# Second layer's memory heads of a two-layer encoder: TensorE's order written out, values in passes of two tiles, and copies first in the stage of sums

## The chip, the cores and the metric

The kernel runs on one core of one Trainium2 chip, as one launch. The metric is the device time of a run in microseconds (us); a lower time is better. The kernel before takes 1526.08 us, the median of three runs (1525.7 to 1526.91).

## The reference

A trunk of two layers over 1024 tokens of width 1024, with 256 memory tokens beside them, all in float32. The first layer has global, windowed and memory heads, the second has neighbourhood and memory heads. What matters here is the second layer:

```python
h = rmsnorm(x, norm_gain[l])
qc, kc, vc, qm, gate = split_cols(h @ w_in_odd[o], SPLIT_ODD)   # 16 heads of 64, 4 of 128, a gate of 1536
yc = neighborhood_attn(qc, kc, vc, rpb_c[o])
ym = memory_attn(qm, mk, mv)           # 4 heads of 128 against 256 memory tokens
y = concat([yc, ym]) * silu(gate)
x = x + y @ w_out_odd[o]

def memory_attn(q, mk, mv):
    s = einsum('bshd,bmhd->bhsm', q, mk) * 128 ** -0.5
    p = softmax(s, axis=-1)
    return einsum('bhsm,bmhd->bshd', p, mv)
```

## The kernel before, in words

**Matmuls.** Every matrix product is made of three `fp32r` matmuls on a high and a low half of each operand: high by high, high by low, low by high. The high half is a rounding copy (`copy`, L112, ScalarE), the low half is the value minus it (VectorE or GpSimd). "Projection of a tile" means 128 output features for all tokens: 2 x 8 steps of three matmuls of 512 columns (`token_steps`, L213 to 230, matmul at L224), into a PSUM bank called `pj`. Activations lie in SBUF as `H`, 16 tiles.

**What sets the order.** A scheduler places each engine's instructions by program order and by priorities: `AHEAD` (L31 to 38) gives each phase a table of names with offsets, and `with self.ahead("evict")` (L81) raises what it encloses by that much. `issue_after` ties an instruction behind another one. An engine wrapped in `Pinned` (L51 to 58) keeps its instructions in program order. Work that is to fill gaps is written as generators in `self.waiting`, and `pull(n)` (L203) issues n steps of them behind the last scores or transposes (`self.fence`).

**Stages.** `prep`; the first layer (`l0`); its output projection (`out0`); `front`; `l1`, which calls `odd`; the last output projection (`out1`). The change touches two:

*`front` (L1374 to 1581), the stage of sums.* It projects the second layer's gates and memory queries by pairs of tiles with sums and differences of the operands, so that seven block products stand for eight. Early products (`x`, `z`) and the values of tiles 0 and 1 (`values_of_two`, L402) run while the operands are still being made (`operands`, L1393); at its start the row sums `rows` of the norm are added (L1656, in `done`), while `weights()` (L1504) splits the next weight tiles. Then a loop (L1540 to 1581) goes over seven pairs in the order 0, 1, 2, 5, 6, 3, 4 (5 and 6 are the memory queries). Each pair has four products into the banks `y`, `x`, `y`, `x` and a last one into `z`; `product` is at L1441. Between them ScalarE copies a bank to SBUF (`c22`, `c12`, `c21`, tiles called `P`), under the priority "sink" (20), VectorE adds (`plus`), and `end` (L1444) finishes a block: gates go through tanh, queries are split into halves, and a DMA stores them. `z` is a new allocation of the single bank `pv`; `x` has five banks.

*`odd` (L1770 to 1821), first part: the opening.* Four memory heads run with the projection of values beside them. `values_of_two` projects value tiles 2 and 3 for all tokens (192 matmuls of 256 columns, weights split into two tiles called `v`, bank `pj`); `values` (L373) projects tiles 4 to 7 at once (192 matmuls of 512 columns, weights in `k` and `v` tiles). Both wait as fill, with the query projection `q0` behind them. `mem_att` (L560) does a head in two groups of four 128-token blocks. For each half group, two blocks: scores into a bank `s` (two buffers; L579 to 581), maximum (L583) and its scaling by `-scale` (L591) on VectorE, exponentials on ScalarE (L594), reciprocal (L598), normalisation on GpSimd (L600), then `pull(1)`. For the whole group then, twice: four transposes into a bank `tr` (`flip`, L120), copy to `ph` and difference `pl` (`p_parts`, L481 to 488), `pull(1)`, three products into `pv` (L611 to 613). At the end of a group `pv` is copied to `y`, and at the end of a head `gated_rows` (L476) multiplies by the gate and stores. Nothing holds TensorE's instructions in this order; the scheduler picks them.

*`odd`, second part.* Eight pairs of neighbourhood heads (`near_head`, L1012), each with the projections of the next pair's keys and queries as fill.

**Tiles.** `k` has eight buffers, `q` four, `v` two, `ph` and `pl` four each; the banks `s`, `tr`, `pv`, `pj` two each. The tag `P` is an alias of `k` in this phase.

Of the kernel before, what the change touches and what calls it, by code (L numbers as in the profile page):

```python
# [23 lines left out]
UNIT = 4  # L24

# [35 lines left out]
class Trunk:  # L61
# [8 lines left out]
    def __init__(self, tc, io):  # L70
        self.tc = tc
        self.nc = tc.nc
        self.io = io
        self.n = 0
        self.bufs = {}
        self.pools = {}
        self.alias = {}
        self.raw = False
        self.later, self.waiting, self.copies = None, deque(), deque([], 8)

# [37 lines left out]
    def flip(self, outs_ins):  # L118
        for o, i in outs_ins:
            self.turned = self.fence = self.nc.tensor.transpose(o, i, self.ident)  # L120
# [91 lines left out]

    def token_steps(self, w, nt, moving, cols, sink):  # L213

        nc = self.nc
        ws = [self.wunit(w[nt, :, u * UNIT * 128:(u + 1) * UNIT * 128]) for u in range(KT // UNIT)]
        for c, n in cols:
            a = self.ps("pj")
            for kt in range(KT):
                h, l = ws[kt // UNIT]  # L220
                mh, ml = moving(kt, c, n)
                with self.ahead("proj"):
                    for i, (s, m) in enumerate(((h, mh), (h, ml), (l, mh))):
                        nc.tensor.matmul(a[:, :n], s[:, kt % UNIT, :], m, start=(kt == 0 and i == 0),  # L224
                                         stop=(kt == KT - 1 and i == 2))
                if kt < KT - 1:
                    yield
            with self.ahead("sink"):
                sink(a, c, n)
            yield  # L230
# [142 lines left out]
    def values(self, w, vd, g):  # L373

        nc = self.nc
        hs = [self.st("k", [128, 2, 512], F32R) for _ in range(4)]
        ls = [self.st("v", [128, 4, 512], F32R) for _ in range(2)]
        ws = [(hs[kt // 2][:, kt % 2, :], ls[kt // 4][:, kt % 4, :]) for kt in range(KT)]
        for kt, (h, l) in enumerate(ws):
            with self.ahead("w"):  # L380
                raw = self.wload(w[4 * g:4 * g + 4, :, kt * 128:(kt + 1) * 128].rearrange("h p n -> p h n"))
                self.copy(h, raw)
                (nc.gpsimd if kt % 2 else nc.vector).tensor_tensor(l, raw, h, op=OP.subtract)
        yield
        for b in range(8):
            p = self.ps("pj")
            t = slice(b * 128, b * 128 + 128)
            for kt, (h, l) in enumerate(ws):
                for i, (x, m) in enumerate(((self.h[0], h), (self.h[0], l), (self.h[1], h))):
                    nc.tensor.matmul(p, x[kt][:, t], m, start=(kt + i == 0), stop=(kt == KT - 1 and i == 2))  # L390
                if kt % 4 == 3:
                    yield
            for e in range(2):
                o = self.st("ph", [128, 2, 2, 2, 64], F32R)
                src = p[:, e * 256:(e + 1) * 256].rearrange("p (j h d) -> p j h d", j=2, h=2)
                with self.ahead("evict"):
                    self.copy(o[:, :, :, 0, :], src)
                    nc.vector.tensor_tensor(o[:, :, :, 1, :], src, o[:, :, :, 0, :], op=OP.subtract)
                    nc.sync.dma_start(vd[2 * g + e][:, :, b, :].rearrange("j p n -> p j n"),
                                      o.bitcast(F32).rearrange("p j h e d -> p j (h e d)"))  # L400

    def values_of_two(self, w, vd, tag, bank, out, pieces=1):  # L402
# [5 lines left out]
        for k in range(0, KT, 2):  # L408
            h, l = hs[k // 2], ls[k // 2]
            with self.ahead("w"):  # L410
# [4 lines left out]
                (nc.vector if pieces > 1 else nc.gpsimd).tensor_tensor(l4, raw, h4, op=OP.subtract)  # L415
        yield
        for b in range(0, 8, 2):
            p = self.ps(bank[b // 2 % len(bank)])
            for e in range(2):
                t = slice((b + e) * 128, (b + e) * 128 + 128)  # L420
                for kt in range(KT):
                    for i, (x, m) in enumerate(((0, hs), (0, ls), (1, hs))):
                        self.last = nc.tensor.matmul(p[:, 256 * e:256 * e + 256], self.h[x][kt][:, t], m[kt // 2][:, kt % 2, :],
                                                     start=e + kt + i == 0, stop=kt == KT - 1 and i == 2,
                                                     skip_group_check=True)
                    if kt % 4 == 3 and (e == 0 or kt < KT - 1):
                        yield
# [8 lines left out]
            yield  # L436
# [123 lines left out]
    def mem_att(self, q, kv):  # L560
        nc = self.nc
        scale = 128.0 ** -0.5
        qh, ql = q
        kh, kl = kv[:, 0, :], kv[:, 1, :]
        vh, vl = (kv[:, i, :].rearrange("p (c d) -> p c d", c=2) for i in (2, 3))
        y = self.st("yb", [128, T])
        wide = "p_sa" in self.bufs
        nb = 4 if wide else 2
        behind = list(self.copies) if wide else []
        for g in range(2):  # L570
            pt = self.st("P", [128, 4, MEM])
            st = self.tiny()
            for i in range(0, 4, nb):
                s = self.ps("sa", (128, T)) if wide else self.ps("s")
                with self.ahead("score"):
                    for b in range(nb):
                        q = slice((g * 4 + i + b) * 128, (g * 4 + i + b + 1) * 128)
                        o = s[:, b * MEM:(b + 1) * MEM]
                        nc.tensor.matmul(o, qh[:, q], kh, start=True, stop=False)  # L579
                        nc.tensor.matmul(o, qh[:, q], kl, start=False, stop=False)  # L580
                        self.fence = nc.tensor.matmul(o, ql[:, q], kh, start=False, stop=True)
                with self.ahead("exp"):
                    nc.vector.tensor_reduce(st[:, i:i + nb], s.rearrange("p (b k) -> p b k", b=nb), axis=AX.X,  # L583
                                            op=OP.max)
                    blk = g * 4 + i
                    raw = self.raw
                    if raw:
# [1335 lines left out]
```

## Time and profile before

| | |
|---|---|
| median of three runs | 1526.08 us (1525.7 to 1526.91) |
| the profiled execution's own time | 1532.29 us |
| its span | 1530.5 us |
| instructions in the span | 24962 |
| TensorE busy | 1484.7 us, 8221 matmuls and transposes |
| VectorE busy | 1051.3 us |
| ScalarE busy | 828.6 us |
| GpSimd busy | 665.1 us |
| mean granted TensorE clock | 0.99 |

How to read it: the profile shows one execution, with its span counted from the first to the last instruction; the execution's own time is 1.8 us more. "PE" is TensorE's matmuls, "PEld" its weight loads, "DVE" VectorE, "ACT" ScalarE, "POOL" GpSimd, "SP" the engine that issues most DMAs. A row of a waits view names the instruction that came after idle time of its engine (engine, output, line), what ended that time (engine, output, line), the idle time in us, how often, and the longest. A row of a windows view gives a stretch in us from the span's start, its length, and for PE, PEld, DVE, ACT and POOL the busy time and the number of instructions; then the granted TensorE clock as a share of full speed, the DMA engines' busy share, and GB/s. A row of a timeline gives start and duration in us, engine, line, operation, output and inputs, and in brackets a wait and what ended it. In these views `front` runs from about 785 to 968, the opening to about 1081, the neighbourhood heads follow.

### The profile page before, as it was taken

What the parts mean: (1) busy time and instruction counts of PE and PEld (TensorE: products, weight loads), DVE (VectorE), ACT (ScalarE), POOL (GpSimd) and SP (SyncE); (2) the same over time, 40 slices, a digit from 0 to 9 for tenths busy, and PEclk for the clock granted to TensorE, in tenths of its full rate; (3) what the DMA queues carried; (4) which work ended last, traced back from release to release, by engine and by line L of the source; (5) the groups of instructions that cost most, each with busy time, mean ns of one, the idle gap of its engine ahead of it and who ended that gap; (6) DMA issues with size and microseconds to landing.
All of it is one profiled execution on the core that took longest, in us unless ns stands there. A gap on an engine that the chain in (4) does not pass through costs nothing.

```text
span 1530.5 us, 24962 instructions
## 1 busy us (share of the span) xinstructions
PE 1484.7 (97%) x8221; PEld 1273.2 (83%) x8221; DVE 1051.3 (69%) x2263; ACT 828.6 (54%) x1822; POOL 665.1 (43%) x790
## 2 busy tenths in 40 slices
PE   9999999999999999999999999988999999999997
PEld 8798898988888788778878777977788888888886
DVE  6687777677676688776578865444477777777754
ACT  7743665655665456554454543443366666666552
POOL 1323547456654555433440001242255566664355
PEclk9999999999999999999999999999999999999998
DMA  8866324232323323287552434674555566678834
GB/s 291 287 163 183 98 70 138 83 118 86 108 90 103 111 84 121 80 283 250 193 171 83 163 116 137 218 236 149 175 166 183 185 206 204 205 214 292 297 121 136
DMA packets 166817, 252.47 MB, mean 165 GB/s; under 512 B 14752, under 2 KB 97952, under 8 KB 165664
## 3 DMA queue, kind: packets, MB, share of 16 engines
q1 hardware_dynamic: 166256, 250.80, 50.9%
q8 instruction: 65, 1.06, 0.3%
q14 instruction: 64, 0.52, 0.1%
q10 hardware_dynamic: 432, 0.09, 0.0%
HBM read 164.32 MB, written 74.45 MB: 156 GB/s over the span
## 4 chain that ended last, share of the span: by engine, by line
PE 82%; DMA 6%; DVE 5%; ACT 2%; issue 2%; POOL 2%; SPq 0%; POOLq 0%; ACTq 0%; DVEq 0%
PE pj L224 27%; PE tr L120 8%; PE pv L995 4%; PE pj L1198 3%; PE x L1441 3%; PE pv L1034 3%; PE sa L1198 3%; PE pj L784 3%; PE tr L1198 2%; PE s L1198 2%; PE pj L390 2%; PE y L1441 2%; PE pv L1441 2%; PE sa L962 2%; PE sa L963 2%
## 5 line engine op out<-in xcount | busy, mean ns | idle before, releaser
L224 PE MATMUL pj<-H,wh 128*128 128x512 f32 x1280 | 423.1, 411 | 1.2 <-DVE vt L313 0.9
L224 PE MATMUL pj<-H,wl 128*128 128x512 f32 x640 | 251.9, 394 | 0.0
L112 ACT ACTIVATE ph<-tr 128x512 fp32r<-128x512 f32 (+2 forms) x336 | 179.7, 539 | 130.8 <-PE tr L120 125.3
L224 PEld LDWEIGHTS pj<-H,wh 128*128 128x128 f32 x1280 | 220.4, 189 | 34.2 <-DVE vt L313 1.2
L487 DVE TENSOR_TENSOR pl<-tr,ph 128x512 fp32r<-128x512 f32 (+2 forms) x336 | 204.8, 615 | 49.7 <-ACT ph L112 47.6
L142 POOL TENSOR_SCALAR wh<-wraw 128x512 fp32r<-128x512 f32 x78 | 51.5, 663 | 284.5 <-DMA g<-P 160.9
L224 PEld LDWEIGHTS pj<-H,wl 128*128 128x128 f32 x640 | 120.2, 188 | 27.7
L112 ACT ACTIVATE wh<-wraw 128x384 fp32r<-128x384 f32 (+1 forms) x162 | 88.6, 552 | 94.3 <-PE tr L1198 16.0
L144 POOL TENSOR_TENSOR wl<-wraw,wh 128x512 fp32r<-128x512 f32 x82 | 106.8, 1304 | 29.9 <-ACT wh L112 25.7
L120 PE MATMUL tr<-ident,P 128*128 128x128 f32 x752 | 115.2, 273 | 1.5 <-DVE pl L487 0.9
L1152 POOL TENSOR_TENSOR wl<-wraw,wh 128x384 fp32r<-128x384 f32 x56 | 61.0, 1089 | 116.7 <-ACT wh L112 108.6
L970 POOL TENSOR_SCALAR P<-P,st 128x1024 f32<-128x1024 f32 x64 | 75.8, 1187 | 66.5 <-DVE st L969 66.4
L1065 POOL TENSOR_SCALAR pn<-pn,st 128x384 f32<-128x384 f32 (+1 forms) x128 | 73.4, 576 | 68.2 <-DVE st L1064 38.2
L1063 ACT ACTIVATE pn<-pn,st 128x384 f32<-128x384 f32 (+1 forms) x128 | 75.1, 587 | 42.6 <-DVE st L1062 36.8
L120 PEld LDWEIGHTS tr<-ident,P 128*128 128x128 f32 x752 | 88.6, 140 | 10.2 <-DVE pl L487 2.1
L968 ACT ACTIVATE P<-sa,st 128x1024 f32<-128x1024 f32 x64 | 71.5, 1117 | 43.3 <-DVE st L967 23.7
L967 DVE TENSOR_REDUCE st<-sa 128x1 f32<-128x1024 f32 x64 | 77.5, 1218 | 12.1 <-PE sa L963 9.4
L784 PE MATMUL pj<-ah,H 128*128 128x256 f32 x384 | 72.7, 286 | 1.0 <-DVE H L729 0.9
L1152 DVE TENSOR_TENSOR wl<-wraw,wh 128x384 fp32r<-128x384 f32 (+1 forms) x64 | 46.7, 730 | 30.4 <-ACT wh L112 30.1
L1059 DVE CUSTOM_DVE_ANT_0 pn<-s,bm 128x384 f32<-128x384 f32 x96 | 53.1, 554 | 20.2 <-PE tr L120 14.5
L995 PE MATMUL pv<-ph,va 128*128 128x256 f32 x256 | 66.6, 285 | 0.0
L995 PE MATMUL pv<-pl,va 128*128 128x256 f32 x256 | 65.8, 284 | 0.0
(502 smaller groups left out, 3912.8 us busy)
## 6 DMA issues: line engine op xcount, KB each, us to landing
wraw<-w_o SPq DMA_DIRECT2D x62, 256.0 KB, 3.7
y<-yb SPq DMA_DIRECT2D x24, 512.0 KB, 3.4
wraw<-s SPq DMA_DIRECT2D x64, 192.0 KB, 3.2
y<-sg SPq DMA_DIRECT2D x23, 512.0 KB, 3.6
wraw<-w_e SPq DMA_DIRECT2D x44, 256.0 KB, 3.0
k<-k SPq DMA_DIRECT2D x42, 256.0 KB, 4.3
wraw<-w_mem SPq DMA_DIRECT2D x32, 256.0 KB, 4.4
v<-v SPq DMA_DIRECT2D x8, 1024.0 KB, 5.1
```

The lines of the kernel that those rows point to most:

```text
L112: return self.nc.scalar.activation(out, in_, AF.Copy, scale=scale)
L120: self.turned = self.fence = self.nc.tensor.transpose(o, i, self.ident)
L144: e.tensor_tensor(lf, raw, hf, op=OP.subtract)
L224: nc.tensor.matmul(a[:, :n], s[:, kt % UNIT, :], m, start=(kt == 0 and i == 0), stop=(kt == KT - 1 and i == 2))
L487: nc.vector.tensor_tensor(pl[:, :n], tr[:, :n], ph[:, :n], op=OP.subtract)
L784: self.last = nc.tensor.matmul(a[:, b * 256:(b + 1) * 256], x[kt][:, t], w, start=(kt + b + i == 0), stop=(kt == KT - 1 and i == 2), skip_ ...
L967: nc.vector.tensor_reduce(st[:, 0:1], s, axis=AX.X, op=OP.max, negate=True)
L970: self.normal = nc.gpsimd.tensor_scalar(pt, pt, st[:, 2:3], 0.5, op0=OP.mult, op1=OP.mult)
L995: nc.tensor.matmul(o[:, :256], v[:, c + k, kv, :], part[:, k * 256:(k + 1) * 256], start=(c + k == 0 and part is parts[0]), stop=(c + k == ...
L1152: engine.tensor_tensor(lf, raw, hf, op=OP.subtract)
L1198: last = nc.tensor.matmul(bank, s[:, k, :], y[3 * u + k][m][:, cols], start=start and u + k + e == 0, stop=u == 1 and k + e == 4, skip_gro ...
L1441: self.last = nc.tensor.matmul(bank, ws[s][:, k, :], b[k][m], start=start and k + i == 0, stop=k == UNIT - 1 and i == 2, skip_group_check= ...
```

## The change

**Opening.** A new function `opening` takes the place of the first part of `odd`. TensorE is wrapped in `Pinned`, so that its instructions stand in the written order: scores of group 0; then for each group n the scores of group n + 1, the transposes and the products of group n. Behind each half group of scores and behind each set of transposes stands fill for `SLOT` = 5800 columns of matmul (a generator step now yields the columns that it issued, and `self.due` carries the rest over). Fill is, in order: the query projection `q0`; three value passes of two tiles (`values_of_two` for tiles 2 and 3 with weights in `v`; 4 and 5 in `k`, in two pieces; 6 and 7 in `v` again); the key projection `k0`; the query projection `q1`. A pass's weights are loaded and split one pass ahead. `values` is gone. The low halves of value weights are made on VectorE (before: on GpSimd for tiles 2 and 3, on both in turn for 4 to 7).

**Queries.** The factor 128^-0.5 is now applied to the memory queries where `front` stores them (`end`), so the exponential takes no scale, the maximum is negated as it is made, and the scaling on VectorE (L591) goes. Queries are loaded by groups of 512 columns, two groups ahead.

**Near heads.** What `opening` has made for the first pair is handed over; `q1` is used for the second pair, and the five steps of fill that the first pair had beside its own (`pull(5)`) go.

**Front.** `weights()` is tied behind the addition of the row sums (`self.squares`). The copies `c22`, `c12` and `c21` get the priority "evict" (500) for "sink" (20). For the pairs 5 and 6 the bank of the last product is a buffer of `x` for `pv`. The low halves of the early value weights stay on VectorE, now by an argument.

`mem_att` itself loses its narrow form (the first layer still calls it) and is cut into `mem_norm`, `mem_flips` and `mem_pv`. The diff, cut to its core:

```diff
+SLOT = 5800
...
     def token_steps(self, w, nt, moving, cols, sink):
-        ws = [self.wunit(w[nt, :, u * UNIT * 128:(u + 1) * UNIT * 128]) for u in range(KT // UNIT)]
+        ws = self.ready.pop(nt, None) or self.units(w, nt)
...
-                        nc.tensor.matmul(a[:, :n], s[:, kt % UNIT, :], m, start=(kt == 0 and i == 0),
+                        self.pe.matmul(a[:, :n], s[:, kt % UNIT, :], m, start=(kt == 0 and i == 0),
...
-                    yield
+                    yield 3 * n
...
-    def values(self, w, vd, g):
...
-    def values_of_two(self, w, vd, tag, bank, out, pieces=1):
+    def values_of_two(self, w, vd, tag, bank, out, pieces=1, low=None):
...
-                (nc.vector if pieces > 1 else nc.gpsimd).tensor_tensor(l4, raw, h4, op=OP.subtract)
+                (low or nc.gpsimd).tensor_tensor(l4, raw, h4, op=OP.subtract)
...
@@ front @@
             if kind == "mem":
-                self.split(o[:, 0, :], o[:, 1, :], p)
+                h, l = (o[:, i, :] for i in range(2))
+                self.copy(h, p, 128.0 ** -0.5)
+                nc.vector.scalar_tensor_tensor(l, p, 128.0 ** -0.5, h, op0=OP.mult, op1=OP.subtract)
...
-                    weights()
+                    with tc.issue_after(self.squares.ins):
+                        weights()
...
-            y, z = self.ps("y"), self.ps("pv")
+            y, z = self.ps("y"), self.ps("pv" if j < early else "x")
...
-            with self.ahead("sink"):
+            with self.ahead("evict"):
                 self.copy(c22, y)
...
-            with self.ahead("sink"):
+            with self.ahead("evict"):
                 self.copy(c12, x)
...
+            with self.ahead("evict"):
+                self.copy(c21, x)
             with self.ahead("sink"):
-                self.copy(c21, x)
                 plus(c22, x)
...
@@ done @@
-                        nc.vector.tensor_tensor(rows1, sums[0], sums[1], op=OP.add)
+                        self.squares = nc.vector.tensor_tensor(rows1, sums[0], sums[1], op=OP.add)
...
+    def opening(self, w, kvd, vd, mqd, gate, yd):
+        nc, tc = self.nc, self.tc
+        self.pe = Pinned(tc, nc.tensor)
+        with self.ahead("first"):
+            kvm = {0: self.load("k", kvd[0], (128, 4, MEM))}
+            load = lambda n: self.load("q", mqd[n // 2][:, :, n % 2 * 512:n % 2 * 512 + 512].rearrange("i p n -> p i n"), (128, 2, 512))
+            qs = deque(load(n) for n in range(2))
...
+        of_two = lambda k, tag, pieces: self.values_of_two(w[O_V + k:O_V + k + 2], vd[k // 2], tag, ("pj",), "ph", pieces, nc.vector)
+        def work():
+            a, b, c = of_two(2, "v", 1), of_two(4, "k", 2), of_two(6, "v", 1)
+            q0 = lazily("q0", lambda: self.q_pair(w, O_Q))
+            first = next(q0)
+            next(a)
+            yield first
+            yield from q0
+            next(b)
+            yield from a
+            next(c)
+            yield from b
+            made["bm"] = [self.near_bias(i) for i in range(2)]
+            k0 = lazily("k0", lambda: self.k_pair(w, O_K))
+            self.ready[O_K] = self.units(w, O_K)
+            yield from c
+            made["v"] = self.load("v", vd[0][0], (128, 8, 256)).rearrange("p b (h d) -> p b h d", h=2)
+            self.ready[O_Q + 1] = self.units(w, O_Q + 1)
+            yield from k0
+            yield from lazily("q1", lambda: self.q_pair(w, O_Q + 1))
+        todo = work()
+        def fill(cols):
+            self.due += cols
+            while self.due > 0:
...
+                self.due -= n
+        fill(16 * 1536)
+        def scores(n):
...
+            for i in range(0, 4, 2):
+                s = self.ps("s")
...
+                with self.ahead("exp"):
+                    nc.vector.tensor_reduce(st[:, i:i + 2], s.rearrange("p (b k) -> p b k", b=2), axis=AX.X, op=OP.max,
+                                            negate=True)
+                    for b in range(2):
+                        nc.scalar.activation(pt[:, i + b, :], s[:, b * MEM:(b + 1) * MEM], AF.Exp,
+                                             bias=st[:, i + b:i + b + 1], accum_out=st[:, 8 + i + b:9 + i + b])
+                    self.mem_norm(pt, st, i, 2)
+                fill(SLOT)
...
+        pt = scores(0)
+        for n in range(8):
...
+            now, pt = pt, scores(n + 1) if n < 7 else None
+            o = self.ps("pv")
+            for c in range(2):
+                parts = self.mem_flips(now, c)
+                fill(SLOT)
+                self.mem_pv(o, kvm[h], c, parts)
+            with self.ahead("close"):
+                self.copy(y[:, g * 512:(g + 1) * 512], o)
+            if g:
+                self.gated_rows(gate(8 + h), 8 + h, y, yd)
+        while not ("q1" in made):
+            fill(1)
...
+        self.pe = nc.tensor
+        return made
...
@@ odd @@
-        self.waiting += [self.values_of_two(w[O_V + 2:O_V + 4], vd[1], "v", ("pj",), "ph"), self.values(w[O_V:], vd, 1)]
...
+        made = self.opening(w, kvd, vd, mqd, gate, yd)
+        now = [made[k] for k in ("bm", "k0", "v", "q0")]
         side = self.weight_sums(self.io["w_oo"], sd, "mk", nc.gpsimd)
-        for h in range(4):
-            y = self.mem_att(mqs.pop(0), kvm)
...
         for j in range(8):
...
-                    now = qkv(j + 1)
+                    now = qkv(j + 1, None if j else made["q1"])
...
-            if j == 0:
-                self.pull(5)
```

167 lines of the change are left out of this document (78 added, 89 removed).

## The prediction, on record before the changed kernel had run

> **What bounds the kernel now.** I read the page first, then busy time by stage, then TensorE's waits inside the two stages that the change touches, then the granted clock around those waits.
>
> ```profile
> span 1530.5 us, 24962 instructions
> ...
> PE 1484.7 (97%) x8221; PEld 1273.2 (83%) x8221; DVE 1051.3 (69%) x2263; ACT 828.6 (54%) x1822; POOL 665.1 (43%) x790
> ```
>
> TensorE is busy in 97% of the span, so nothing can be won but its idle time and the time it runs at a lower clock. The table by stage says where that is. Its first columns are the stretch, its length, and PE busy; PEclk is the granted clock.
>
> ```profile
> 785.00:830.00 45.00, 42.05 (x271) 37.62 (x270) 33.43 (x64) 20.21 (x37) 3.15 (x2) 0.96 0.43 141
> 830.00:968.00 138.00, 133.29 (x571) 107.50 (x570) 91.58 (x144) 62.84 (x110) 9.21 (x8) 0.99 0.42 140
> 968.00:1081.00 113.00, 103.68 (x598) 89.72 (x597) 48.83 (x99) 44.26 (x125) 32.25 (x47) 0.95 0.58 190
> 1081.00:1120.00 39.00, 37.76 (x187) 31.15 (x186) 21.36 (x71) 18.30 (x46) 17.71 (x25) 1.00 0.63 191
> 1120.00:1300.00 180.00, 180.00 (x1007) 156.04 (x1006) 134.90 (x450) 117.48 (x291) 109.27 (x159) 1.00 0.61 189
> ```
>
> The first two rows are the stage of sums (`front`), the third is the second layer's opening: its memory heads with the value projections. TensorE is idle for 2.95 + 4.71 us in the one and 9.32 us in the other. From 1120 on it is idle for nothing: those neighbourhood heads are bound by TensorE itself. The first heads (1081 to 1120) lose 1.24 us. What ended the idle time, first in the stage of sums, then from 968 to 1120:
>
> ```profile
> PE x L1441 <- ACT P L112: 2.7, 1, 2.7
> PE pv L1441 <- ACT P L112: 1.9, 2, 1.0
> PE pv L265 <- DVE rows L1656: 1.1, 1, 1.1
> PE y L423 <- DVE H L58: 1.0, 1, 1.0
> ```
>
> ```profile
> PE s L579 <- ACT k L594: 6.9, 3, 4.4
> PE tr L120 <- POOL k L600: 1.6, 2, 1.0
> PE s L1052 <- DMA k<-k: 0.6, 1, 0.6
> PE s L579 <- DMA k<-kv: 0.6, 1, 0.6
> PE s L1051 <- DMA k<-k: 0.3, 1, 0.3
> ```
>
> In the opening, scores wait for a PSUM bank that the exponentials still read (6.9 us in three waits), transposes wait for GpSimd's normalised probabilities (1.6). There is a second loss that the busy time hides, since matmuls at half clock count as busy:
>
> ```profile
> 787.10:790.60 3.50, 2.42 (x16) 1.85 (x15) 1.98 (x4) 2.01 (x4) 1.13 (x1) 1.00 0.82 243
> 790.60:794.00 3.40, 3.40 (x10) 2.63 (x9) 3.02 (x15) 0.39 (x1) 0.00 (x0) 0.50 0.86 268
> ...
> 852.00:855.40 3.40, 1.07 (x5) 0.88 (x6) 3.40 (x6) 1.80 (x4) 0.00 (x0) 1.00 0.51 159
> 855.40:858.80 3.40, 3.40 (x10) 2.64 (x9) 2.99 (x6) 0.63 (x1) 0.00 (x0) 0.50 0.23 77
> 1008.90:1012.30 3.40, 1.07 (x8) 0.79 (x7) 2.67 (x8) 2.78 (x11) 0.70 (x1) 1.00 0.46 157
> 1012.30:1015.70 3.40, 3.40 (x13) 2.88 (x13) 3.40 (x8) 2.52 (x5) 3.40 (x6) 0.52 0.33 81
> ...
> 1036.20:1039.60 3.40, 1.36 (x6) 1.36 (x7) 1.60 (x5) 2.44 (x10) 1.89 (x4) 0.52 0.32 107
> 1039.60:1043.00 3.40, 3.40 (x13) 2.82 (x12) 3.02 (x8) 1.73 (x8) 0.80 (x2) 0.50 0.50 158
> ```
>
> Each stretch with a stall is followed by one at a granted clock of 0.50 or 0.52. Half of the busy time at half clock is lost: 1.7 us at 790.6, 1.7 at 855.4, and in the opening 3.40 x 0.48 + 1.36 x 0.48 + 3.40 x 0.50 = 4.0 us. So the opening loses 9.3 + 4.0 = **13.3 us**, and the stage of sums 7.7 + 3.4 = **11.1 us**.
>
> **The change, part by part.** First the opening. TensorE's instructions now stand in a written order: scores of group n+1, then transposes and products of group n, with 5800 columns of fill (value passes, then projections) behind each half group of scores and each set of transposes. In the program order of the changed kernel, scores of one group and transposes of the same group have work of TensorE between them that I count, at 0.12 and 0.23 us a matmul (rows below), as some 10 us for the first group and 18 for the later ones, where the longest of the three old waits was 4.4 us. A PSUM bank of scores is used again one group half later, with 2.9 us of fill in between. I count all 13.3 us as gone, before what is new.
>
> New is, first, the cost of narrower passes. Two passes of two tiles replace one of four: 384 matmuls of 256 columns for 192 of 512. Start to start:
>
> ```profile
> 969.83 1.60 PE L423 MATMUL pj<-v,H 128*128 128x256 f32 x12
> 971.27 0.28 PE L581 MATMUL s<-k,q 128*128 128x256 f32 x1
> ...
> 1046.02 0.62 PE L390 MATMUL pj<-k,H 128*128 128x512 f32 x2
> 1046.48 0.39 PE L390 MATMUL pj<-v,H 128*128 128x512 f32 x1
> 1046.70 0.62 PE L390 MATMUL pj<-k,H 128*128 128x512 f32 x2
> ```
>
> Twelve narrow ones take 971.27 - 969.83 = 1.44 us, 0.120 each; three wide ones 1046.70 - 1046.02 = 0.68, 0.227 each. 384 x 0.120 - 192 x 0.227 = 46.1 - 43.5 = **+2.6 us**, wholly on the path. [...]
>
> Second, one stall that the fixed order brings. The third value pass (tiles 6 and 7) puts its weights into the two `v` buffers of the first, so its four ScalarE copies wait until that pass has made its last matmul. They stand in ScalarE's queue ahead of the copy `ph` of the next transposes, with two evictions among them, and behind those transposes stand only 12 fill matmuls (12 x 0.120 = 1.4 us). The pieces:
>
> ```profile
> 960.17 2.18 ACT L112 ACTIVATE v<-wraw 128x512 fp32r<-128x512 f32 x4
> ...
> 979.00 0.59 ACT L112 ACTIVATE ph<-tr 128x512 fp32r<-128x512 f32 x1
> ...
> 982.13 0.38 ACT L112 ACTIVATE ph<-pj 128x256 fp32r<-128x256 f32 x1 [0.49 <-DVE ph L433]
> ```
>
> ```profile
> 979.62 0.69 DVE L487 TENSOR_TENSOR pl<-tr,ph 128x512 fp32r<-128x512 f32 x1 [0.32 <-ACT ph L112]
> ...
> 981.68 0.42 DVE L433 TENSOR_TENSOR ph<-pj,ph 128x256 fp32r<-128x256 f32 x1 [0.52 <-ACT ph L112]
> ```
>
> 2.18 + 2 x 0.38 + 0.59 = 3.5 us until `ph` is there and 0.69 more for `pl`: 4.2 us. TensorE reaches the third product, which needs `pl`, after 1.4 us of fill and some 0.8 us of transposes and two products (estimate from 0.227 a wide matmul). It idles about 2 us; with the hand-over between engines I take **+2.5 us** (bounds 1 and 4.5). Such a stall is as long as the one before 1012.3, so it may halve the clock for the next 3.4 us; 1.7 us at two chances in three, **+1.1**.
>
> For all other transposes the chain is 0.59 + 0.69 = 1.3 us, and behind an eviction pair 2 x (0.38 + 0.42) = 1.6 us more, 2.9 in all. There the fill is mostly 24 matmuls, 2.9 us, with the products before `pl` on top. That hides it. If the cover is gone, each of 16 waits costs up to 1.5 us. The lower halves of the value weights move from GpSimd to VectorE; VectorE is busy 48.83 of 113 us in the stage, so they lie beside other work. On the DMA queue the loads of later groups' queries stand behind stores that wait for evictions, but each has a group of time (14 us) to land. The key copies that follow (`k<-k`, 0.9 us of waits) remain about as late, since the next heads start right behind k's second half: 0. Their fill is 78 matmuls now against 81, no difference.
>
> Opening: -13.3 + 2.6 + 2.5 + 1.1 = **-7.1 us**.
>
> Now the stage of sums. (a) At its start TensorE waits for the row sums. VectorE does a weight's low half first, then the addition:
>
> ```profile
> 785.52 1.54 DVE L58 TENSOR_TENSOR wl<-wraw,wh 128x512 fp32r<-128x512 f32 x1 [0.17 <-ACT wh L112]
> ...
> 788.49 0.69 DVE L1656 TENSOR_TENSOR rows<-vt,ph 128x512 f32<-128x512 f32 x1 [0.83 <-ACT ph L1212]
> ```
>
> The change puts that low half behind the addition, which so starts up to 1.5 us earlier; the wait is 1.1 us. It goes, and with it the half clock: 1.1 + 1.7 = 2.8. But the third piece of the value weights is now loaded behind four other loads, and TensorE may wait for it: I take -2.5 (bounds 0 and -3.8, with the next wait of 1.0 gone as well). (b) At 854 the product waits for the copy of its bank:
>
> ```profile
> 851.42 0.63 ACT L112 ACTIVATE wh<-wraw 128x512 fp32r<-128x512 f32 x1 [2.10 <-PE y L1441]
> 853.16 0.63 ACT L112 ACTIVATE t<-P 128x512 fp32r<-128x512 f32 x1 [1.12 <-DVE P L58]
> 853.70 0.58 ACT L112 ACTIVATE P<-x 128x512 f32<-128x512 f32 x1
> ```
>
> The copy `P<-x` stands behind `t<-P`, which waits for VectorE. With a higher priority it stands ahead and starts at about 852.0: -1.6 of the 2.7, and with the rest of the stall 1.1 us long the half clock goes: -1.7. (c) For the two late pairs the last product gets a bank of its own (`x` for `pv`): both waits of `pv`, -1.9. Against it, VectorE is busy nearly all the time around 850, and TensorE, earlier than before, may meet operands not yet done: +0.7 (estimate; bounds 0 and 3). Stage of sums: -2.5 - 1.6 - 1.7 - 1.9 + 0.7 = **-7.0 us**.
>
> **Sum.** -7.1 - 7.0 = -14.1 us. The profiled execution took 1532.29 us, 1.8 more than its span, and would take 1518.2. It is 6.2 us slower than the median of the runs; taking the difference over, 1526.08 - 14.1 = **1512.0 us**.
>
> **Rivals.** *Slower: the fixed order exposes each hand-over.* Before, the scheduler could put other matmuls into a late hand-over; a written order can't. If at each of the 16 transposes ScalarE and VectorE have a weight split or an exponential pair ahead of `ph`, TensorE waits each time. Without the one stall counted above the change gives -7.0 - 13.3 + 2.6 = -17.7, so it turns at 17.7 / 16 = 1.1 us a wait; at 1.5 us it gives 1526.1 - 17.7 + 24 = 1532. For it speaks the chain of up to 2.9 us against 2.9 of fill; against it, ScalarE is busy 44.26 of 113 us. Chance 0.09.
>
> *VectorE bounds the stage of sums*, and what is won at its start is lost again at 850: only (c) and the opening remain, 1526.1 - 7.1 - 1.9 = 1517. For it: VectorE 33.43 of 45 us. Chance 0.17.
>
> *No stall at the weights' copies*: 1512.0 - 3.6 = 1508.4. Chance 0.13.
>
> *The stall doesn't halve the clock*: 1512.0 - 1.1 = 1510.9. Against it stands the stretch 1008.9, with 1.07 us of work in it, and 0.52 after it. Chance 0.08. [...]
>
> *That the change doesn't do what it says* has no room: the program order shows the written sequence in place and the copy ahead of `t<-P`.
>
> **Chances.** Forecast 0.53; the others as given. The range must take in the VectorE case and the ends of the stall: 1503 to 1520. Below lies the case that all 24.4 us but the split come back (1504.3 and a little luck), above it the slower rival. A measurement can tell about 0.2%, 3 us, from no change. Faster by more 0.87, within 0.05 (the slower rival at about 1.1 us a wait), slower 0.08.
>
> **What would show it.** After the change: no wait of scores for exponentials; one wait of `pv` for `ph` or `pl` in the opening, some 2 us long, where the third pass's weights are copied; wide-pass matmuls gone and 192 more of 256 columns at 0.120; no wait of `pv` for `P`; the stretch after the row sums at full clock. I am wrong if waits for `ph` or `pl` come at most transposes, or if the heads after the opening are no longer free of idle time.

## The result, and the profile after

| | before | changed |
|---|---|---|
| median of 4 runs each | 1526.49 us (1525.7 to 1528.58) | 1518.87 us (1515.65 to 1520.51) |
| ratio | | 0.9948, 95% interval 0.9927 to 0.9968 |
| profiled execution | 1532.29 us | 1515.65 us |

The change is faster, by 7.6 us between the medians; forecast were 14.1. Two repeats, on two chips, gave 0.9933 (0.9922 to 0.9945) and 0.9948 (0.9931 to 0.9965). Between the two profiled executions, however, 16.6 us went. That difference between 16.6 and 7.6 turned out to be the point of the case.

First the page of the changed kernel: TensorE's busy time is 5 us lower although it makes 192 matmuls more.

```profile
span 1513.9 us, 25309 instructions
...
PE 1479.4 (98%) x8413; PEld 1281.5 (85%) x8413; DVE 1046.0 (69%) x2255; ACT 830.2 (55%) x1822; POOL 659.9 (44%) x782
```

The table by stage, over the stretches that correspond to the first four rows shown of before (two of the stage of sums, the opening, the first heads; the last one holds more work than its counterpart, 216 matmuls for 187):

```profile
784.60:829.60 45.00, 42.69 (x281) 38.45 (x280) 35.06 (x69) 21.23 (x40) 2.50 (x2) 1.00 0.43 145
829.60:963.30 133.70, 130.31 (x563) 104.76 (x562) 90.30 (x144) 61.66 (x107) 3.85 (x4) 1.00 0.43 143
963.30:1077.90 114.60, 112.71 (x841) 106.62 (x839) 47.40 (x91) 47.05 (x127) 32.07 (x47) 1.00 0.65 213
1077.90:1120.00 42.10, 39.92 (x216) 33.74 (x217) 27.86 (x101) 24.96 (x63) 23.40 (x35) 1.00 0.50 146
```

The granted clock (the share of full speed at which TensorE ran) is 1.00 in all four; it was 0.96, 0.99 and 0.95 in the first three. The opening is idle for 1.9 us instead of 9.3, the stage of sums for 2.3 + 3.4 = 5.7 instead of 7.7. What ended the idle time of TensorE, first in the stage of sums, then from 963 to 1130:

```profile
PE x L1413 <- ACT P L114: 2.1, 1, 2.1
PE y L398 <- DVE H L59: 0.9, 1, 0.9
PE tr L122 <- DVE rq_y L247: 0.6, 1, 0.6
PE pv L269 <- DVE rows L1632: 0.5, 1, 0.5
PE x L1413 <- ACT wh L114: 0.5, 1, 0.5
PE pv L1413 <- DVE t L59: 0.5, 2, 0.3
...
PE x L1413 <- DVE P L1445: 0.3, 1, 0.3
```

```profile
PE pv L59 <- ACT ph L114: 1.3, 1, 1.3
PE s L1023 <- DMA k<-k: 0.8, 1, 0.8
PE s L1024 <- DMA k<-k: 0.7, 2, 0.5
PE tr L122 <- POOL pn L1037: 0.6, 1, 0.6
PE pv L59 <- DVE pl L462: 0.5, 1, 0.5
```

In the opening no scores wait for exponentials and no transposes for GpSimd any more. One wait is left, of the products for `ph` and `pl`, at the place the prediction named. In the stage of sums the longest wait, of `x` for the copy `P`, is still there. The two waits of `pv` for `P` are gone, and two shorter waits of `x` (for `wh` and `P`, 0.5 and 0.3) stand at their places.

The same work can be timed from three rows of each kernel: first product of the stage of sums, first memory scores, first scores of the ninth neighbourhood head. Of before, then of after:

```profile
785.35 0.39 PE L1441 MATMUL x<-H,wh 128*128 128x512 f32 x1
...
968.87 0.28 PE L579 MATMUL s<-k,q 128*128 128x256 f32 x1
...
1242.42 0.28 PE L1051 MATMUL s<-k,q 128*128 128x256 f32 x1
```

```profile
784.62 0.39 PE L1413 MATMUL x<-H,wh 128*128 128x512 f32 x1
...
963.26 0.40 PE L59 MATMUL s<-k,q 128*128 128x256 f32 x2
...
1227.12 0.28 PE L1023 MATMUL s<-k,q 128*128 128x256 f32 x1
```

The stage of sums took 183.5 us and takes 178.6; the opening with eight heads took 273.6 and takes 263.9. That is 14.6 us, in these two executions.

### The profile page after: what moved, and what is told of

It reads as the page before. It is cut to its first block, busy times and chain, and to the rows that moved or that the text cites. A ratio compares the mean times of both kernels' runs of the same rounds, so it can differ in the third digit from the quotient of the medians.

```text
span 1513.9 us, 25309 instructions
## 1 busy us (share of the span) xinstructions
PE 1479.4 (98%) x8413; PEld 1281.5 (85%) x8413; DVE 1046.0 (69%) x2255; ACT 830.2 (55%) x1822; POOL 659.9 (44%) x782
## 3 DMA queue, kind: packets, MB, share of 16 engines
q8 instruction: 66, 1.08, 0.3%
## 4 chain that ended last, share of the span: by engine, by line
PE 86%; DMA 4%; DVE 4%; ACT 2%; issue 1%; POOL 1%; SPq 0%; POOLq 0%; ACTq 0%; DVEq 0%
PE pj L228 27%; PE tr L122 8%; PE pj L59 6%; PE pv L967 4%; PE pj L1170 4%; PE sa L1170 4%; PE x L1413 3%; PE pv L1006 3%; PE pj L756 3%; PE tr L1170 3%; PE s L1170 2%; PE sa L934 2%; PE sa L935 2%; PE y L1413 2%; PE pv L1170 2%; PE pv L1413 1%
## 5 line engine op out<-in xcount | busy, mean ns | idle before, releaser
L228 PE MATMUL pj<-H,wh 128*128 128x512 f32 x1198 | 397.2, 412 | 0.6 <-DVE vt L299 0.2
L228 PE MATMUL pj<-H,wl 128*128 128x512 f32 x599 | 235.8, 394 | 0.0
L228 PEld LDWEIGHTS pj<-H,wh 128*128 128x128 f32 x1198 | 205.3, 189 | 30.3 <-issue 0.8
L228 PEld LDWEIGHTS pj<-H,wl 128*128 128x128 f32 x599 | 112.5, 188 | 26.2
```

Of the source, the lines that this page charges most:

```text
L228: self.pe.matmul(a[:, :n], s[:, kt % UNIT, :], m, start=(kt == 0 and i == 0), stop=(kt == KT - 1 and i == 2))
```

## The experiments

Ratios are to the kernel before, run beside it on the same chip. "Granted clock" is the mean over a run's span.

**1. Both kernels again.** No edit.

> The kernel before once more, unchanged, to see what its executions other than the profiled one look like. Between the two profiled executions 16.6 us went (1532.29 to 1515.65), between the medians 7.6. Theory 1: the half-clock stretches behind the stalls are an accident of the one profiled execution; most executions have the same idle time but few of those stretches. Then: ratio 1.000, mean granted clock 0.994 or more in most runs (0.990 in the profiled one), and in this profile 17 us of TensorE idle time in the stage of sums and the opening as before, with at most one or two stretches at 0.50 there. Theory 2 (as the prediction had it): each of the longer stalls brings its half-clock stretch, so the clock is 0.990 again and four stretches at 0.50 stand at the same places; the missing gain is then to be sought in the changed kernel.

Measured: 1526.27 us, ratio 0.9990 (0.9977 to 1.0003). Clocks from 0.992 to 0.996, median 0.994. In its profile the stage of sums took 181.5 us and the opening with eight heads 268.7. So another execution of the same kernel was 6.9 us shorter over the same work than the one the prediction was made from. Its waits in the opening:

```profile
PE s L579 <- ACT k L594: 3.9, 4, 2.4
PE tr L120 <- POOL k L600: 2.0, 2, 1.0
```

3.9 us for 6.9: the idle time of the opening, 9.3 us in the first profile, is 6.1 here. And two half-clock stretches (3.4 us at a granted clock of 0.5) stand in these stages, at 858 and 1015, where the first profile has five of 3.4 us. Theory 1 holds for the clock; that the idle time would be the same was wrong.

> The changed kernel once more, to get a second profile and a narrower ratio; its four runs lay 4.9 us apart. Theory 1: ratio 0.995, about -7.5 us, mean clock 0.994 to 0.996 as in the runs before; the idle places of the profile stay the same. Theory 2: the clock is lower in the slower runs than in the faster ones, at least by 0.001 for each 1.7 us.

> The changed kernel once more, beside the next three on one chip. Ratio to before 0.993 to 0.995; the stall for ph and pl at 996 is 1.3 + 0.5 us again, as in all profiles with the written order.

Measured: 1517.57 us, 0.9933 (0.9922 to 0.9945), and 1520.18 us, 0.9948 (0.9931 to 0.9965). The stages took 179.8 + 263.5 and 179.4 + 264.7 us. The stall for `ph` and `pl` is 1.33 + 0.47 us in all three profiles. In `after_again` theory 2 fits: the two slowest of its five runs have the lowest clocks, 0.993 and 0.992; the ratio of theory 1, 0.995, lies outside the interval.

**2. Each half of the change alone.** `front_only` is the kernel before with the edits of the stage of sums; `opening_only` is the changed kernel without them:

```diff
-                    weights()
+                    with tc.issue_after(self.squares.ins):
+                        weights()
...
-            y, z = self.ps("y"), self.ps("pv")
+            y, z = self.ps("y"), self.ps("pv" if j < early else "x")
...
-            with self.ahead("sink"):
+            with self.ahead("evict"):
                 self.copy(c22, y)
```

(and `c12`, `c21` in the same way).

> The kernel before with only the edits of the stage of sums (weights behind the addition, copies first, x for pv). Theory 1: idle time alone counts; the profile of the change shows 5.7 us idle in that stage for 7.7, so -2 us, ratio 0.9987. Theory 2 (the prediction): -7.0 us, ratio 0.9954, as the two half-clock stretches go too.

> The changed kernel with the edits of the stage of sums undone: the opening alone. Theory 1: idle 9.3 to 1.9 us, +2.6 us for the narrower passes, +0.9 for the first heads: -4 us, ratio 0.9974. Theory 2 (the prediction): -7.1 us, ratio 0.9953.

Measured: the stage of sums alone 0.9985 (0.9974 to 0.9996), -2.3 us. The opening alone 0.9963 (0.9946 to 0.9980), -5.7 us. Forecast were 7.0 and 7.1: the first is out by far. The second lies within its interval, but so does the rival's 4 us (0.9974), so the time alone doesn't choose between them. In `front_only`, which has the old opening, the opening's profile shows no half-clock stretch at all, and waits for exponentials of 3.1 us and for GpSimd of 1.2. So in three executions the old opening had three, one and no half-clock stretches, and 9.3, 6.1 and 5.1 us idle.

**3. The copy's priority undone.** In the changed kernel:

```diff
-            with self.ahead("evict"):
+            with self.ahead("sink"):
                 self.copy(c22, y)
```

(and `c12`, `c21`).

> The changed kernel with the three copies of the stage of sums back at the priority sink; on ScalarE only the order of P<-x and t<-P at about 850 is changed. Theory 1: the copy P<-x doesn't wait for its place in ScalarE's queue but for its own buffer, which VectorE's second difference P<-P,P sets free; the priority won 0.5 us of a 2.7 us wait. Then the wait of x for P goes from 2.15 to about 2.7 us, ratio to the kernel before 0.9937. Theory 2 (the prediction): the priority is worth 1.6 us and most of a half-clock stretch, so +2.5 us, ratio 0.995.

Measured: 0.9954 (0.9936 to 0.9971), which the time alone can't tell from the change. Its profile can:

```profile
PE x L1413 <- ACT P L114: 2.5, 1, 2.5
```

2.5 us, theory 1 had 2.7; the three profiles of the change have 2.15, 2.04 and 2.00. The priority is worth at most about half a microsecond, not 1.6. The trace of the changed kernel says what the copy waits for. ScalarE, then VectorE:

```profile
849.94 0.60 ACT L114 ACTIVATE P<-x 128x512 f32<-128x512 f32 x1 [1.17 <-DVE P L59]
```

```profile
847.35 0.69 DVE L1461 TENSOR_TENSOR wraw<-wq,wq 128x512 f32<-128x512 f32 x1 [1.30 <-DMA wq<-w_o]
847.96 0.68 DVE L59 SCALAR_TENSOR_TENSOR wq<-vt,wq 128x512 f32<-128x512 f32 x1
848.56 0.69 DVE L59 TENSOR_TENSOR t<-P,t 128x512 fp32r<-128x512 f32 x1
849.16 0.68 DVE L59 TENSOR_TENSOR P<-P,P 128x512 f32<-128x512 f32 x1
```

`P<-x` is at the head of ScalarE's queue and waits 1.17 us for VectorE: its buffer is one of six called `P`, and the difference at 849.16 is the last reader. That difference stands three instructions behind a sum that waited 1.30 us for a load.

**4. The sum put behind the differences.** In the changed kernel, `diffs` being the list of the differences:

```diff
-                with self.ahead("w"):
+                with self.ahead("w"), tc.issue_after(diffs[-2].ins) if o is s1 and one else nullcontext():
...
-            ws = sums(ws) if j else first
+            ws = sums(ws, j == 1) if j else first
```

> The changed kernel with VectorE's first sum of pair 1's weights put behind the third difference of t4. That sum waits 1.3 us for a load (wq<-w_o), and the difference that frees the copy's buffer stands 3 instructions behind it. Theory 1: the difference ends 2 us earlier, the wait of x for P falls from 2.15 us to under 0.5 and no half-clock stretch stands near 850: -1.8 to -3 us against the changed kernel, ratio to before 0.992. Rival: pair 1's first product takes over the wait, as its weight's low half comes that much later; then 0.9935 and a wait of y for wl near 853.

Measured: 0.9959 (0.9944 to 0.9974), no gain. The waits between 840 and 870:

```profile
PE pv L1413 <- DVE t L59: 1.7, 2, 1.0
PE y L1413 <- ACT wh L114: 0.7, 1, 0.7
PE x L1413 <- ACT P L114: 0.4, 1, 0.4
```

The wait for the copy falls to 0.4, as theory 1 had it, and 1.7 + 0.7 us come in its place, waits for VectorE's next results and for the weights that the sum feeds. 2.8 us for the 2.6 of before this edit (2.15 for `P`, 0.47 for `t`). The rival was right that the wait only moves; most of it came to `pv` and not, as the rival had it, to `y`. The longer of the two waits of `pv`, 1.0 us, ends when VectorE has made `t`, just behind its next sum of weights, which had itself waited for a load:

```profile
858.29 0.69 DVE L1461 TENSOR_TENSOR wraw<-wq,wq 128x512 f32<-128x512 f32 x1 [1.66 <-DMA wq<-w_o]
```

So VectorE's results are what TensorE waits for in both orders, but VectorE isn't simply full there: it stands idle for a load of weights, 1.30 us in the one order and 1.66 in the other. Whether an earlier load would take the wait away was not tried.

**5. The stall at 996.** First the third pass's weights begun four fill steps later, then the same with their copies tied behind the next copy `ph`:

```diff
-            next(c)
+            for _ in range(4):
+                yield next(b)
+            next(c)
             yield from b
```

```diff
+            for _ in range(4):
+                yield next(b)
-            next(c)
+            with tc.issue_after(self.copies[-1].ins):
+                next(c)
             yield from b
```

> The changed kernel with the third pass's weights begun four fill steps later, so that ScalarE has the copy ph of those transposes ahead of the four v copies. Theory: the stall at 996 (1.33 for ph and 0.47 for pl in both profiles of the changed kernel) is those copies; it goes to under 0.3 and the opening has no idle time: -1.8 us, ratio to before 0.992. Rival: the v copies hold the next ph up in the same way, and the stall only moves to the next transposes: no difference, 0.9935.

> The changed kernel, order written out, with the third pass's weights four fill steps later and tied behind the copy ph of the second transposes, which moves the four v copies behind that copy in ScalarE's queue (in the run with the later start alone the scheduler had left them ahead). Theory: the four v copies are the stall; no wait for ph or pl at 996, opening idle under 0.3 us, -1.8 us and about one half-clock stretch in two less: ratio to before 0.991 to 0.9925. Rival: the stall is ph waiting for something else (the two evictions, a buffer); then 1 us or more of it stays.

Measured for the first: 0.9949 (0.9932 to 0.9967) and the same stall, 1.33 + 0.47. It didn't test the theory: the scheduler left the four copies ahead of `ph` on ScalarE. ScalarE of the changed kernel, which is the same there:

```profile
992.96 1.16 ACT L114 ACTIVATE v<-wraw 128x512 fp32r<-128x512 f32 x2 [1.01 <-PE pj L59]
994.02 0.36 ACT L114 ACTIVATE ph<-pj 128x256 fp32r<-128x256 f32 x1
994.28 1.14 ACT L114 ACTIVATE v<-wraw 128x512 fp32r<-128x512 f32 x2
995.32 0.37 ACT L114 ACTIVATE ph<-pj 128x256 fp32r<-128x256 f32 x1
995.59 0.59 ACT L114 ACTIVATE ph<-tr 128x512 fp32r<-128x512 f32 x1
```

With the copies tied behind, 0.9912 (0.9893 to 0.9930), 1515.18 us beside 1520.18 for the changed kernel on the same chip. ScalarE, then TensorE, at the same place:

```profile
996.43 0.59 ACT L114 ACTIVATE ph<-tr 128x512 fp32r<-128x512 f32 x1
998.82 0.60 ACT L114 ACTIVATE ph<-tr 128x512 fp32r<-128x512 f32 x1 [1.80 <-issue]
999.32 2.18 ACT L114 ACTIVATE v<-wraw 128x512 fp32r<-128x512 f32 x4
```

```profile
995.43 1.67 PE L59 MATMUL pj<-k,H 128*128 128x256 f32 x12
997.08 0.73 PE L59 MATMUL pv<-ph,k 128*128 128x512 f32 x2
```

No wait is left. The four copies were the stall. The opening with eight heads takes 261.0 us; in the seven profiles that have the stall it takes 263.0 to 264.7, mean 263.6. That is 2.6 us of the 5.0 between the medians. The rest goes with a higher mean clock of these four runs (0.9965 for 0.9940), of which the stall explains little: half clock stands behind it in 2 of the 7 profiles (0.54 in `c_later`, 0.53 in `after_third`).

**6. The order left to the scheduler.** In the changed kernel, twice, on two chips:

```diff
-        self.pe = Pinned(tc, nc.tensor)
```

> The changed kernel with TensorE's order in the opening left to the scheduler, everything else (passes of two tiles, scores a group ahead, loads, fill) as changed. Theory: the program order is what takes the idle time away, and the written order adds little: within 2 us of the changed kernel, ratio 0.992 to 0.995. Rival 1: the written order is what does it; without it the waits of scores for exponentials come back, 3 to 6 us, ratio 0.996 to 0.997. Rival 2 (the prediction's slower rival, in reverse): the scheduler puts work into the stall at 996, 1.8 us faster than the changed kernel.

> The kernel with TensorE's order left to the scheduler once more. Theory: what it won (0.9915) is real: no idle time in the opening, about 3 us shorter from the first memory scores to the first near head than the changed kernel, and a little more by fewer half-clock stretches: ratio 0.991 to 0.992. Rival: it was a lucky draw of the clock (mean 0.996); then 0.993, level with the changed kernel of this call.

Measured: 0.9915 (0.9898 to 0.9931), then 0.9909 (0.9890 to 0.9927), 1514.2 us beside 1520.18 for the changed kernel. The opening's row in the table by stage (111.7 us, no idle time, against 114.6 in the changed kernel) and TensorE at the place of the stall:

```profile
964.00:1075.70 111.70, 111.70 (x838) 106.73 (x837) 46.36 (x90) 45.67 (x125) 31.93 (x47) 1.00 0.67 209
```

```profile
995.28 0.27 PE L122 MATMUL tr<-ident,k 128*128 128x128 f32 x1
995.31 2.76 PE L398 MATMUL pj<-k,H 128*128 128x256 f32 x21
```

The scheduler puts 21 fill matmuls behind those transposes where the written order has 12, and so covers the same late `ph`. Rival 2 was right in kind. The opening with eight heads takes 260.1 us in both profiles, 3.5 less than with the stall; the 6.0 us between the medians again include a higher clock (0.9956 for 0.9940). So the written order wins nothing, and what it costs, it costs by the four copies: with them moved (experiment 5) it is 261.0 us, nearly as short as the free order.

**7. Scores not in advance.** The kernel of 6 with

```diff
-        pt = scores(0)
         for n in range(8):
...
-            now, pt = pt, scores(n + 1) if n < 7 else None
+            now = scores(n)
```

> The kernel with the order left to the scheduler, and in addition scores of each group directly ahead of its own transposes, not a group in advance. Theory: scores in advance are what took away the waits for exponentials and normalisation; without them 2 to 5 us of TensorE idle time stand in the opening again, ratio 0.993 to 0.996. Rival: the fill by 5800 columns in program order is enough by itself, since the scheduler can move it; then as the kernel with scores in advance, 0.9915.

Measured: 0.9913 (0.9895 to 0.9932), 1515.31 us, no idle time of TensorE in the opening (114.1 us busy of 114.1). Up to the ninth neighbourhood head it is 259.8 us against the 260.1 of experiment 6. The rival was right: with the scheduler free, scores in advance bring nothing. What keeps TensorE busy then has no run of its own. Larger steps of fill as such don't explain it. In the three profiles of the old opening the narrow pass, whose step is 12 matmuls or 3072 columns, has a single wait of 0.16 or 0.17 us. The other waits stand behind it: at the change of passes, where for 6.4 to 7.4 us no value matmul runs (1006.2 to 1013.6 in the first profile) and scores wait 1.9 to 2.4, and in the wide pass, whose step is 6144 columns, more than 5800. The wait at the change of passes, in the first profile:

```profile
1011.37 0.38 PE L579 MATMUL s<-k,q 128*128 128x256 f32 x1 [2.33 <-ACT k L594]
```

The changed kernel splits each pass's weights a pass ahead, and VectorE's scaling of the maxima is gone; no run undoes one of these alone.

## Why the prediction was right in direction and range, and nearly twice too large

**The clock: the step that failed most.** The prediction took 7.4 us of half clock from one profile, let the change remove all of it and bring back 1.1, net -6.3. It also called the profiled execution 6.2 us slower than the median and "took the difference over". Those 6 us were the same thing: that execution had more half-clock stretches in the opening (three, against one and none) and longer stalls there (9.3 us idle, against 6.1 and 5.1) than the other two profiled with the old opening.

Over 60 runs of the kernel before on three chips the mean granted clock is 0.9931, over 15 of the changed kernel 0.9943. 0.0012 of 1520 us is 1.8 us: by this estimate so much does the clock give, where 6.3 were counted. It is a rough figure, since the twelve runs of `before_again` alone have 0.9941. The mean times are 1527.1 and 1518.9 us, 8.2 apart. Without the clock 6.4 us remain; the terms of the forecast without the clock sum to -14.1 + 6.3 = -7.8. That these two are so close is in part luck: in the opening the idle time was taken 2.5 us too large and the narrower passes 2.2 too dear (both below), which nearly cancels.

Why one profile isn't enough is best seen in the written order's stall, 1.33 + 0.47 us in two executions of which only one loses clock afterwards. The changed kernel, then the kernel with the third pass begun later:

```profile
995.30:998.70 3.40, 1.99 (x12) 1.49 (x13) 2.08 (x4) 1.11 (x4) 1.67 (x2) 1.00 0.93 275
998.70:1002.10 3.40, 3.40 (x28) 3.27 (x27) 0.69 (x1) 0.49 (x2) 2.47 (x4) 1.00 0.82 273
```

```profile
994.50:997.90 3.40, 1.60 (x8) 0.89 (x8) 2.93 (x6) 1.73 (x4) 0.71 (x2) 1.00 0.64 215
997.90:1001.30 3.40, 3.40 (x19) 3.40 (x18) 0.69 (x1) 0.60 (x1) 3.13 (x4) 0.54 0.96 287
```

1.99 us busy of 3.4, and the clock stays; 1.60, and the next stretch has 0.54. The 24 fill matmuls behind it take 4.62 us there and 3.11 in the changed kernel:

```profile
998.13 3.11 PE L59 MATMUL pj<-k,H 128*128 128x256 f32 x24
```

```profile
998.18 4.62 PE L59 MATMUL pj<-k,H 128*128 128x256 f32 x24
```

Ahead of its last 20 us the profile of before shows the granted clock falling to 0.5 at 684.75, 790.57, 855.42, 1012.43 and 1036.33, that of the changed kernel at 60.62, 149.36 and 685.26. Within each profile these starts lie whole multiples of 3.41 us apart: 105.82, 64.85, 157.01 and 23.90 us are 31, 19, 46 and 7 of them, 88.74 and 535.90 are 26 and 157. The half clock lasts one such step, behind 1036.33 two. Seven of these nine steps at half clock follow a step with 1.80 to 2.52 us idle, the other two follow 1.08 (before 790.57) and 1.53 (before 685.26). All other steps of the two profiles have at most 1.49 us idle, and the clock behind them is 1.00. In `c_later` 1.80 us of idle time lie in the 3.40 before 997.9. In the changed kernel, counted in steps from its half clock at 685.26, the same stall is divided: 0.97 us lie in the step before 995.87 and 0.84 in the one behind it. That the loss depends on this division is the author's estimate from these two profiles; no run moved a stall against the steps.

The wait for `P` near 850 was followed by half clock in 9 of the 13 profiles where it was 1.6 us or longer (0.50 in `before` and 0.54 in `after_again`, but 1.00 in the changed kernel's first profile), the stall at 996 in 2 of 7, the start of the stage of sums with the old order in 2 of 3.

**Opening, idle time (-9.3).** The mechanism was right: the waits for exponentials and for normalised probabilities are all gone. The size was that of one execution; three profiles of the old opening show 9.3, 6.1 and 5.1, mean 6.8. Most of the excess is one wait of scores, 4.4 us at 1038, where the other two profiles have 1.2 and 0.9. Of the kernel before, VectorE's scaling of the maxima, which the exponentials wait for, and GpSimd beside it:

```profile
1033.31 3.83 DVE L591 TENSOR_SCALAR st<-st 128x2 f32<-128x2 f32 x2
```

```profile
1033.32 3.72 POOL L144 TENSOR_TENSOR wl<-wraw,wh 128x512 fp32r<-128x512 f32 x3
```

The first of the two scalings took 3.75 us, as long as GpSimd's three differences; the others in this opening took 0.15 to 0.77, and the longest in the other two profiles 1.32. The change drops this instruction, which the prediction didn't count as a gain; what that alone is worth was not run. That the written order and the scores in advance bring the gain was wrong: experiments 6 and 7 do without either.

**Narrower passes (+2.6).** From start to start over all rows of the value matmuls, 69.6 us (`front_only`, no clock lost) became 70.1: about +0.4. The prediction priced both kinds in unbroken runs, and the old opening's weren't: there the scheduler mixed them with scores and transposes.

**The stall (+2.5).** Right in place and cause, 1.8 us in size, 1.33 before `ph` and 0.47 before `pl` (the chain of copies took 996.18 - 992.96 = 3.2 us where 3.5 were worked out). The chance that it halves the clock, two in three, looks too high with 2 of 7.

**The rival of exposed hand-overs** didn't come: one of 16 transposes waits, the one that was named. In small it holds: the kernel without the written order is 6.0 us faster than with it on the same chip, 3.5 of them in the traces.

**First heads (0).** The copies `k<-k` now cost 0.8 + 0.7 us where they cost 0.6 + 0.3, and transposes wait 0.6 for GpSimd: the idle time went from 1.24 to 2.18 us, +0.9.

**Stage of sums (-7.0).** Measured -2.3 alone.
- (a) The wait for the row sums fell from 1.08 to 0.52 us. With the low half out of the way the addition starts 2.6 us after the first product instead of 3.1, because VectorE then waits for GpSimd, which the prediction didn't look at. Of the changed kernel:

```profile
787.21 0.69 DVE L1632 TENSOR_TENSOR rows<-vt,ph 128x512 f32<-128x512 f32 x1 [1.70 <-POOL vt L1186]
```

  The next wait, of transposes for `rq_y`, 0 to 1.2 us before, is 0.6 to 1.7 now. The idle time of the first 45 us was 2.95, 3.54 and 2.22 in three profiles of the old order and is 2.31, 2.60 and 2.72 in the three of the change. The half-clock stretch after it is gone in all 11 profiles with the edit (granted clock 1.00 from 784.6 to 829.6 in the first of them).
- (b) The step that failed: "with a higher priority it stands ahead and starts at about 852.0". It stands ahead, and waits there for a buffer. The wait was 2.74, 1.96 and 2.17 us in three profiles of the old stage, and 2.15, 2.04 and 2.00 with the edit: next to nothing (experiment 3: at most half a microsecond), where 1.6 + 1.7 were counted.
- (c) The bank: both waits of 0.97 gone, 0.49 + 0.28 at the same places new: -1.2 for -1.9.
- The rival "VectorE bounds the stage of sums" gave 1517, nearer to the result than the forecast, but its mechanism is only half shown. Nothing won at the start was lost again at 850: at the start little was won, as (a) says. Around 850 TensorE waits for VectorE in both orders of experiment 4, and VectorE there for loads.

## What to carry to other kernels

The same stall of 1.33 + 0.47 us was followed by half clock in 2 of 7 profiles: count a half-clock stretch with a chance taken from several profiles or from the mean clock of many runs, and never take a single profile's losses over to the median. Before an instruction is moved forward in a queue, look at all that it waits for, its own destination buffer first. And when an order is written out by hand, run the same program with the order left free: here the copies that the fixed order couldn't step around cost 2.6 us in the traces, and 5 of the 12.6 us between the medians (1520.18 and 1515.18 us, 1527.76 before), part of it clock that no run ties to them; the free order (0.9915 and 0.9909) and the written one with the copies moved (0.9912) beat both kernels.

## What the runs showed of the hardware that was not expected

In the profiles of before and of the changed kernel the granted clock fell to 0.5 behind steps of 3.41 us that were 0.90 to 1.62 us busy, in seven cases of nine. There is an exception the other way, at the start of the stage of sums: 2.42 us busy of 3.5 before 790.6, eight of the matmuls there with one column, and 0.50 after it, with the old order in two of three profiles. A step of the changed kernel with less, 1.92 us busy of 3.41 before 852.51, was followed by 1.00. Busy time by the profile alone therefore doesn't tell the cases apart; what does was not tried.

A VectorE instruction on two columns took 3.75 us, beside 0.15 for the shortest of its kind in this opening, while GpSimd ran three differences, 3.72 us. It did so in one of three profiles of that opening, and no run tried what held it.
